# Twelve groups of transposes in an encoder layer, moved from TensorE to DMA

## The chip, the core and the metric

The kernel runs on one core of one Trainium2 chip. The core has a matrix engine (TensorE, PE in the profile), a vector engine (VectorE, DVE), a scalar engine (ScalarE, ACT), a general engine (GpSimd, POOL), a sequencer that mostly issues transfers (SyncE, SP), and 16 DMA engines. Operands lie in SBUF, 128 partitions wide; TensorE writes its results to PSUM, and DMA here moves between HBM and SBUF, or within SBUF. The metric is device time in microseconds of one execution, lower is better.

## What is computed

One layer of a bidirectional encoder on 256 tokens of width 2048, all in float32. Two kinds of attention run side by side on the same projection, and their outputs are gated, merged, projected and followed by an MLP:

```python
h = rms_norm(x, norm_mix_pre[l])
proj = jnp.einsum('bsd,dc->bsc', h, w_in[l])
qa, ka, va, qn, kn, vn, gates = jnp.split(proj, split_at, axis=-1)
...
oa = diff_attention(qa, ka, va, lam)
oa = (rms_norm(oa, subln_w[l]) * (1.0 - lambda_init)).reshape(B, S, DA_WIDTH)
on = neighbourhood_attention(...)
g_a, g_b = jnp.split(jax.nn.sigmoid(gates), N_BRANCHES, axis=-1)
mixed = (g_a * jnp.einsum('bsc,cd->bsd', oa, w_branch_a[l])
         + g_b * jnp.einsum('bsc,cd->bsd', on, w_branch_b[l]))
y = jnp.einsum('bsd,de->bse', mixed, w_out[l])
x = x + rms_norm(y, norm_mix_post[l])
h = rms_norm(x, norm_mlp_pre[l])
u = jnp.square(jax.nn.relu(jnp.einsum('bsd,df->bsf', h, w_up[l])))
x = x + rms_norm(jnp.einsum('bsf,fd->bsd', u, w_down[l]), norm_mlp_post[l])
```

There are four differential heads (called a0 to a3 here), whose weights are `softmax(s1) - lam * softmax(s2)` and whose output is 256 wide, and eight neighbourhood heads (n0 to n7), 128 wide, with a bias and a mask on the scores.

## The kernel before

**Numbers.** Products are made of float32 values split in two parts of a shorter float type, a high and a low one (`hi`, `lo`). ScalarE casts the high part and VectorE subtracts it from the value to get the low one (`parts`, L419; for weights `split`, L138 and L146). A product is then two or three matmuls: for the projections to q and k high times both parts at once (L224, 512 columns) and low times the high part (L226, 256 columns); elsewhere high-high, high-low and low-high (`product3`, L424).

**Projections.** `wgroup` (L215) computes q or k for 512 columns of the weight in four chunks of 4 x 128 rows: 16 pairs of L224 and L226 for one chunk. `agroup` (L258) does v. A chunk's weights are one load of 1 MB on SyncE's queue (L116), then split; raw, high and low parts each have three buffers (pool `wp`, L58). The order is q, k, v for a0 and a1, then for a2 and a3, then for n0 to n3, then for n4 to n7, then the gates, the branch products (`ba`, `bb`), `w_out` and the MLP.

**Heads.** A head is a generator that runs in pieces between the chunks of later projections: `advance` (L204) is called once for a chunk and runs one piece of the head whose turn it is (two from L644 on). A differential head (`diff_head`, L483) has four pieces: the scores and the weights `p`, 2 x 128 x 256, written by L518; `p` transposed (`p_transposed`, L469, called at L522); the product with v (tile `do`), its norm and the scaled output `on` (L544, tile `don` in the profile); and `on` transposed on TensorE (L549, tile `dot`), then scaled and split into `oaT` (L558, L559), which the branch product `ba` reads much later. A neighbourhood head (`na_head`, L564) has three: weights `p` (last written by L597), `p` transposed, and the product with v (tile `no`) with its split into `onT`.

A transposed tile takes four TensorE instructions of 128x128 each, in one PSUM bank, out of which ScalarE and VectorE split it (L421, L422) into `pT`. All these pieces use temporary tiles of 2 KB for a partition (`t2k`, L72), of which there are seven.

**The transposes by DMA that exist.** `sent` (L700) and `joined` (L709) transpose two merged tiles at about 470 us: ScalarE splits float32 into two planes of 16 bits (L704), a DMA on SyncE's queue transposes the planes (L706), and ScalarE joins the two 16-bit halves again (L711). These handle 128 x 2 x 512 values at a time.

**Order.** Nobody writes out the order on each engine. A planner sets it before the run, from the dependences and its own estimate of durations (L36); each engine and each DMA queue then works strictly in that order. Where the program has `issue_after`, an order is forced; the parts touched here have none.

Of the kernel before, what the change touches and what calls it, by code (L numbers as in the profile page):

```python
# [11 lines left out]
F32 = mybir.dt.float32  # L12
F32R = mybir.dt.float32r
U16 = mybir.dt.uint16
AF = mybir.ActivationFunctionType
ALU = mybir.AluOpType
AX = mybir.AxisListType

P = 128
D = 2048  # L20
T = 256
# [30 lines left out]
def encoder_layer(ctx: ExitStack, tc: tile.TileContext, a, out):  # L52
    nc = tc.nc
# [12 lines left out]
    def page(shape, dt, name):  # L66
        return pages.tile(shape, dt, tag="pg", name=name)
# [4 lines left out]
    def t2k(name, dt=F32):  # L72
        return tmp.tile([P, 2, T], dt, tag="t2k", name=name, bufs=7)

    def bank(name, big=False):
        if big:
            return mm.tile([P, 512], F32, tag="mm", name=name)
        return ms.tile([P, 512], F32, tag="ms", name=name)

    def small(w, name):  # L80
        return tiny.tile([P, w], F32, tag=f"s{w}", name=name)
# [13 lines left out]
    def inv_rms(ss, n, name, r=None):  # L95

        w = ss.shape[1]
        ms_ = small(w, f"{name}_m")
        scaled[0] = nc.vector.tensor_scalar(
            ms_, ss, 1.0 / n, EPS, op0=ALU.mult, op1=ALU.add  # L100
        ).ins
        if r is None:
            r = small(w, f"{name}_r")
        nc.gpsimd.tensor_tensor(r, ms_, expo[:, :w], op=ALU.pow)
        return r
# [51 lines left out]
    at = 0  # L157
# [7 lines left out]
    ident = const.tile([P, P], F32, name="ident")  # L165
# [253 lines left out]
    def parts(dst, at, src):  # L419
        hi, lo = dst  # L420
        nc.scalar.copy(hi[at], src)  # L421
        nc.vector.tensor_sub(lo[at], src, hi[at].bitcast(F32))  # L422

    def product3(ps, stat, s_at, mov, m_at, start, stop):  # L424

        for i, (sp, mp) in enumerate(((0, 0), (0, 1), (1, 0))):
            nc.tensor.matmul(
                ps, stat[sp][s_at], mov[mp][m_at], start=start and i == 0, stop=stop and i == 2
            )
# [39 lines left out]
    def p_transposed(p, name):  # L469

        pt = bank(f"{name}_pt")
        for kt in range(2):
            for t in range(2):
                nc.tensor.transpose(
                    pt[:, kt * T + t * P : kt * T + (t + 1) * P],
                    p[:, t, kt * P : (kt + 1) * P],
                    ident,
                )
        r = [t2k(f"{name}_pT{i}", F32R) for i in range(2)]
        parts(r, slice(None), pt.rearrange("p (k q) -> p k q", k=2))  # L480
        return r

    def diff_head(h, qT, kT, v, hl, sc):  # L483
        p = t2k(f"dp{h}")
        for t in range(2):
            s = bank(f"ds{h}{t}")
            for c in range(2):
                product3(
                    s[:, c * T : (c + 1) * T],
                    qT,  # L490
                    (slice(None), hl * 2 + c, slice(t * P, (t + 1) * P)),
                    kT,
                    (slice(None), hl * 2 + c),
                    True,
                    True,
                )
            nb = small(2, f"dnb{h}{t}")
            nc.vector.tensor_reduce(
                nb, s.rearrange("p (c k) -> p c k", c=2), axis=AX.X, op=ALU.max, negate=True
            )  # L500
            nbs = small(2, f"dnbs{h}{t}")
            nc.vector.tensor_scalar_mul(nbs, nb, sc[t])
            e = t2k(f"de{h}{t}")
            z = small(2, f"dz{h}{t}")
            for c in range(2):
                nc.scalar.activation(
                    e[:, c],
                    s[:, c * T : (c + 1) * T],
                    AF.Exp,
                    bias=nbs[:, c : c + 1],  # L510
                    scale=sc[t],
                    accum_out=z[:, c : c + 1],
                )
            rz = small(2, f"drz{h}{t}")
            nc.vector.reciprocal(rz, z)
            nc.vector.tensor_mul(rz[:, 1:2], rz[:, 1:2], lam)
            nc.vector.tensor_scalar_mul(e[:, 1], e[:, 1], rz[:, 1:2])
            nc.vector.scalar_tensor_tensor(  # L518
                p[:, t], e[:, 0], rz[:, 0:1], e[:, 1], op0=ALU.mult, op1=ALU.subtract
            )  # L520
        yield True
        pT = p_transposed(p, f"d{h}")  # L522
        yield True
        o = bank(f"do{h}")
        for t in range(2):
            for kt in range(2):
                product3(
                    o[:, t * T : (t + 1) * T],
                    pT,
                    (slice(None), kt, slice(t * P, (t + 1) * P)),  # L530
                    v,
                    (slice(None), kt, slice(hl * T, (hl + 1) * T)),
                    kt == 0,
                    kt == 1,
                )
        ss = small(2, f"dss{h}")
        on = t2k(f"don{h}")
        for t in range(2):
            nc.scalar.activation(
                on[:, t], o[:, t * T : (t + 1) * T], AF.Square, accum_out=ss[:, t : t + 1]  # L540
            )
        r = inv_rms(ss, 2 * HD, f"dr{h}")
        for t in range(2):
            nc.vector.tensor_scalar_mul(on[:, t], o[:, t * T : (t + 1) * T], r[:, t : t + 1])  # L544
        yield True
        pt = bank(f"dot{h}")
        for eb in range(2):
            for t in range(2):
                nc.tensor.transpose(  # L549
                    pt[:, eb * T + t * P : eb * T + (t + 1) * P],  # L550
                    on[:, t, eb * P : (eb + 1) * P],
                    ident,
                )
        ot = page([P, 2, 512], F32R, f"oaT{h}")
        for eb in range(2):
            src = pt[:, eb * T : (eb + 1) * T]
            g = subs[:, eb : eb + 1]
            nc.scalar.activation(ot[:, eb, :T], src, AF.Copy, scale=g)  # L558
            nc.vector.scalar_tensor_tensor(  # L559
                ot[:, eb, T:], src, g, ot[:, eb, :T].bitcast(F32), op0=ALU.mult, op1=ALU.subtract  # L560
            )
            oT["a", h * 2 + eb] = ot[:, eb]

    def na_head(h, qT, kT, v, hl):  # L564
        p = t2k(f"np{h}")
        s = bank(f"ns{h}")
        for t in range(2):
            product3(
                s[:, t * T : (t + 1) * T],
                qT,  # L570
                (slice(None), hl, slice(t * P, (t + 1) * P)),
                kT,
                (slice(None), hl),
                True,
                True,
            )
        b = bias[h // 2][:, h % 2]
        for t in range(2):
            nc.vector.scalar_tensor_tensor(
                p[:, t],  # L580
                s[:, t * T : (t + 1) * T],
                rxs[:, t : t + 1],
                b[:, 2 - 2 * t : 6 - 2 * t].rearrange("p i c -> p (i c)"),
                op0=ALU.mult,
                op1=ALU.add,
            )
        nb = small(2, f"nnb{h}")
        nc.vector.tensor_reduce(nb, p, axis=AX.X, op=ALU.max, negate=True)
        z = small(2, f"nz{h}")
        for t in range(2):  # L590
            nc.scalar.activation(
                p[:, t], p[:, t], AF.Exp, bias=nb[:, t : t + 1], accum_out=z[:, t : t + 1]
            )
        rz = small(2, f"nrz{h}")
        nc.vector.reciprocal(rz, z)
        for t in range(2):
            nc.vector.tensor_scalar_mul(p[:, t], p[:, t], rz[:, t : t + 1])  # L597
        yield True
        pT = p_transposed(p, f"n{h}")
        yield True  # L600
        o = bank(f"no{h}")
        for kt in range(2):
            product3(
                o[:, :T],
                v,
                (slice(None), kt, slice(hl * P, (hl + 1) * P)),
                pT,
                (slice(None), kt),
                kt == 0,
                kt == 1,  # L610
            )
        if h % 2 == 0:
            oT["nt", h // 2] = page([P, 2, 512], F32R, f"onT{h}")
        ot = oT["nt", h // 2][:, h % 2]
        nc.scalar.copy(ot[:, :T], o[:, :T])
        nc.vector.tensor_sub(ot[:, T:], o[:, :T], ot[:, :T].bitcast(F32))
        oT["n", h] = ot
# [802 lines left out]
    for g in range(2):  # L1420
        pr = Products(f"p{g}", (1, 2, 3, 7))
        pr.in_order = True
        for bi, b in enumerate(blocks[g]):
            end = bi == len(blocks[g]) - 1
            for n, (cg, j, seven) in enumerate(down_steps(g, bi)):
# [42 lines left out]
                for which in range(4):  # L1468
# [4 lines left out]
                    if last:  # L1473
                        bank_, t, half = PLAIN[which]
# [65 lines left out]
```

## Time and profile before

| what | us |
|---|---|
| device time, median of 3 runs | 1337.97 (1337.49 to 1337.99) |
| the profiled execution's own time | 1338.14 |
| its span, first to last instruction | 1336.3 |
| PE busy | 1328.3 |
| DVE busy | 1096.0 |
| ACT busy | 747.7 |

The profile is of one execution. Busy times are sums over an engine's instructions without overlaps; PE's matmuls are pipelined, so a matmul's own duration is longer than the distance to the next one's start. The granted clock of TensorE was 0.998 of full speed. The page names instructions by line of the kernel, engine, operation and tiles, with tile numbers left out: `dp`, `do`, `don`, `dot` belong to the differential heads, `np`, `no` to the neighbourhood heads. In timelines, the first column is the start and the second the length in us, and `[x <-ENGINE tile line]` is the idle time before an instruction and what ended it. SPq and ACTq are the queues' issuing instructions.

### The profile page before, as it was taken

The page shows a single profiled execution, that of the slowest core. Times are in us where ns is not written, and L with a number is a line of the kernel's source. Part 1 is how long each engine was busy: PE and PEld are TensorE (multiplying, and loading weights), DVE is VectorE, ACT ScalarE, POOL GpSimd, SP SyncE. Part 2 cuts the span into 40 slices and gives each one's busy share as a digit, 9 for nine tenths or more (in the row PEclk, how much of TensorE's full clock was granted, in tenths as well). Part 3 has the DMA queues.
Part 4 walks back from the last instruction along what each step waited for, and adds up shares of the span by engine and source line. Part 5 has one row for each costly group of instructions (what it writes and reads, how often), then busy time and mean ns, then how long its engine had stood idle before and what let it go on. Part 6 is the DMA issues. An engine that isn't in the chain of part 4 may idle for free.

```text
span 1336.3 us, 16265 instructions
## 1 busy us (share of the span) xinstructions
PE 1328.3 (99%) x6289; PEld 1112.5 (83%) x6289; DVE 1096.0 (82%) x1275; ACT 747.7 (56%) x873; POOL 39.3 (3%) x73
## 2 busy tenths in 40 slices
PE   9999999999999999999999999999999999999998
PEld 8888888888888888888888888888888888888886
DVE  7978766667787889885688999999978888898886
ACT  6655555545545575555475666666555555555542
POOL 0000000000000000000100000000000000000000
PEclk9999999999999999999999999999999999999999
DMA  9874645564564676567658677877797998698995
GB/s 352 264 228 161 195 165 180 179 192 157 189 217 169 213 220 222 189 220 263 231 182 276 238 250 268 306 238 248 250 361 280 395 385 334 248 371 332 358 351 207
DMA packets 118285, 336.90 MB, mean 252 GB/s; under 512 B 20928, under 2 KB 21440, under 8 KB 118208
## 3 DMA queue, kind: packets, MB, share of 16 engines
q1 hardware_dynamic: 98528, 266.92, 57.9%
q10 hardware_dynamic: 12960, 43.26, 8.4%
q0 software_dynamic: 6720, 25.69, 4.9%
q8 instruction: 49, 0.80, 0.2%
q14 instruction: 28, 0.23, 0.0%
HBM read 307.01 MB, written 29.61 MB: 252 GB/s over the span
## 4 chain that ended last, share of the span: by engine, by line
PE 73%; issue 21%; DMA 3%; DVE 1%; ACT 1%; POOL 0%; POOLq 0%; ACTq 0%
PE u L761 23%; PE ga L761 6%; PE gb L761 6%; PE bb L761 3%; PE ba L761 3%; PE y L761 3%; PE qa_p L224 2%; PE ka_p L224 2%; PE kn_p L224 2%; PE qn_p L224 2%; PE qa_p L226 1%; PE qn_p L226 1%; PE ka_p L226 1%; PE kn_p L226 1%; PE vn_p L267 1%
## 5 line engine op out<-in xcount | busy, mean ns | idle before, releaser
L224 PE MATMUL qn_p<-hT,qn_h 128*128 128x512 f32 x128 | 45.9, 400 | 0.0
L224 PE MATMUL kn_p<-hT,kn_h 128*128 128x512 f32 x128 | 45.6, 400 | 0.0
L224 PE MATMUL ka_p<-hT,ka_h 128*128 128x512 f32 x128 | 45.2, 399 | 0.0
L224 PE MATMUL qa_p<-hT,qa_h 128*128 128x512 f32 x128 | 43.8, 400 | 0.4 <-DVE hT L308 0.4
L761 PE MATMUL u<-u_2h,h2T 128*128 128x512 f32 x128 | 44.0, 396 | 0.0
L761 PE MATMUL u<-u_1h,h2T 128*128 128x512 f32 x128 | 43.4, 389 | 0.0
L761 PE MATMUL u<-u_4h,h2T 128*128 128x512 f32 x128 | 43.3, 391 | 0.0
L761 PE MATMUL u<-u_6h,h2T 128*128 128x512 f32 x128 | 41.0, 389 | 0.0
L761 PE MATMUL u<-u_7h,h2T 128*128 128x512 f32 x128 | 41.0, 389 | 0.0
L226 PE MATMUL qn_p<-hT,qn_l 128*128 128x256 f32 x128 | 35.9, 281 | 0.0
L226 PE MATMUL kn_p<-hT,kn_l 128*128 128x256 f32 x128 | 35.7, 280 | 0.0
L226 PE MATMUL ka_p<-hT,ka_l 128*128 128x256 f32 x128 | 35.2, 282 | 0.0
L226 PE MATMUL qa_p<-hT,qa_l 128*128 128x256 f32 x128 | 32.5, 282 | 0.0
L146 DVE TENSOR_TENSOR y_l<-y_w,y_h 128x1024 fp32r<-128x1024 f32 x16 | 19.0, 1220 | 11.9 <-ACT y_h L138 11.9
L224 PEld LDWEIGHTS kn_p<-hT,kn_h 128*128 128x128 f32 x128 | 24.0, 188 | 5.5
L224 PEld LDWEIGHTS qn_p<-hT,qn_h 128*128 128x128 f32 x128 | 24.1, 188 | 5.3
L146 DVE TENSOR_TENSOR kn_l<-kn_w,kn_h 128x1024 fp32r<-128x1024 f32 x16 | 19.0, 1220 | 11.5 <-ACT kn_h L138 11.5
L224 PEld LDWEIGHTS ka_p<-hT,ka_h 128*128 128x128 f32 x128 | 23.9, 188 | 5.3
L761 PEld LDWEIGHTS u<-u_1h,h2T 128*128 128x128 f32 x128 | 24.0, 188 | 5.0
L146 DVE TENSOR_TENSOR vn_l<-vn_w,vn_h 128x1024 fp32r<-128x1024 f32 x16 | 19.0, 1221 | 11.2 <-ACT vn_h L138 11.2
L761 PEld LDWEIGHTS u<-u_7h,h2T 128*128 128x128 f32 x128 | 24.0, 188 | 5.0
L761 PEld LDWEIGHTS u<-u_6h,h2T 128*128 128x128 f32 x128 | 24.0, 188 | 5.0
(1636 smaller groups left out, 4573.1 us busy)
## 6 DMA issues: line engine op xcount, KB each, us to landing
bh<-keeph ACTq DMA_DIRECT2D x30, 512.0 KB, 9.0
bl<-keepl ACTq DMA_DIRECT2D x30, 512.0 KB, 10.9
keeph<-ah POOLq DMA_DIRECT2D x18, 512.0 KB, 3.8
keepl<-al POOLq DMA_DIRECT2D x18, 512.0 KB, 6.5
va_w<-in_w_in SPq DMA_DIRECT2D x8, 1024.0 KB, 6.4
qn_w<-in_w_in SPq DMA_DIRECT2D x8, 1024.0 KB, 5.1
kn_w<-in_w_in SPq DMA_DIRECT2D x8, 1024.0 KB, 5.0
vn_w<-in_w_in SPq DMA_DIRECT2D x8, 1024.0 KB, 5.0
```

What stands on the lines that cost most here:

```text
L146: sub = nc.vector.tensor_sub(lo[part], src, hi[part].bitcast(F32)).ins
L224: nc.tensor.matmul(ps[b], hi[:, k % 4, cs], mv, start=(k == 0), stop=False)
L226: nc.tensor.matmul(ps[b][:, :T], lo[:, k % 4, cs], mv[:, :T], start=False, stop=(k == nk - 1))
L267: nc.tensor.matmul(ps[t], sh, hi[:, k % 4], start=(k == 0), stop=False)
L761: ins = nc.tensor.matmul(self.ps[i], st, mv[:, blk], start=i not in self.begun, stop=last and n == 2).ins
```

## The change

Heads a0 to a3 and n0 to n3 no longer transpose on TensorE. As soon as a tile (`p`, and for a0 to a3 also `on`) is written, `send` has ScalarE copy it into two planes of 16 bits and a DMA on SyncE's queue transpose them. In the piece where TensorE transposed, `received` has ScalarE join the planes again, and `p_received` then splits the joined tile into `hi` and `lo` from SBUF. That is 12 tiles: 2 for each of four differential heads, 1 for each of four neighbourhood heads, with 4 transposes each, 48 in all. Heads n4 to n7 keep `p_transposed`. The transposed `p` lies as (t, k, q) in place of (k, t, q), for all heads, and the products that read it are written for that. Plane, transfer and join each take a `t2k` tile of the same seven.

```diff
-        r = [t2k(f"{name}_pT{i}", F32R) for i in range(2)]
-        parts(r, slice(None), pt.rearrange("p (k q) -> p k q", k=2))
+        r = [
+            t2k(f"{name}_pT{i}", F32R).rearrange("p t (k q) -> p t k q", k=2) for i in range(2)
+        ]
+        parts(r, slice(None), pt.rearrange("p (k t q) -> p t k q", k=2, t=2))
+        return r
+
+    def send(p, name):
+
+        planes = t2k(f"{name}_s").rearrange("p a b -> p (a b)").bitcast(U16)
+        planes = planes.rearrange("p (t h c) -> p t h c", t=2, h=2)
+        got = t2k(f"{name}_g").rearrange("p a b -> p (a b)").bitcast(U16)
+        nc.scalar.copy(planes, p.bitcast(U16).rearrange("p t (c h) -> p t h c", h=2))
+        nc.sync.dma_start(
+            got.rearrange("p (b q) -> p b q", q=P),
+            planes.rearrange("p t h c -> p (t h c)"),
+            transpose=True,
+        )
+        return got
+
+    def received(got, name):
+
+        r = t2k(name)
+        nc.scalar.copy(
+            r.bitcast(U16).rearrange("p t (c h) -> p t h c", h=2),
+            got.rearrange("p (t h c) -> p t h c", t=2, h=2),
+        )
+        return r.rearrange("p t (k q) -> p t k q", k=2)
+
+    def p_received(got, name):
+
+        pT = received(got, f"{name}_pT")
+        r = [
+            t2k(f"{name}_pT{i}", F32R).rearrange("p t (k q) -> p t k q", k=2) for i in range(2)
+        ]
+        parts(r, slice(None), pT)
         return r
...
@@ diff_head
+        got = send(p, f"dp{h}")
         yield True
-        pT = p_transposed(p, f"d{h}")
+        pT = p_received(got, f"d{h}")
         yield True
...
-                    (slice(None), kt, slice(t * P, (t + 1) * P)),
+                    (slice(None), t, kt),
...
+        got = send(on, f"do{h}")
         yield True
-        pt = bank(f"dot{h}")
-        for eb in range(2):
-            for t in range(2):
-                nc.tensor.transpose(
-                    pt[:, eb * T + t * P : eb * T + (t + 1) * P],
-                    on[:, t, eb * P : (eb + 1) * P],
-                    ident,
-                )
+        oT_ = received(got, f"dot{h}")
         ot = page([P, 2, 512], F32R, f"oaT{h}")
         for eb in range(2):
-            src = pt[:, eb * T : (eb + 1) * T]
+            src = oT_[:, :, eb]
...
@@ na_head
+        got = send(p, f"np{h}") if h < 4 else None
         yield True
-        pT = p_transposed(p, f"n{h}")
+        pT = p_received(got, f"n{h}") if got is not None else p_transposed(p, f"n{h}")
         yield True
         o = bank(f"no{h}")
         for kt in range(2):
             product3(
-                o[:, :T],
+                o[:, :T].rearrange("p (t q) -> p t q", t=2),
                 v,
                 (slice(None), kt, slice(hl * P, (hl + 1) * P)),
                 pT,
-                (slice(None), kt),
+                (slice(None), slice(None), kt),
```

More of the change, by code (lines that the diff above doesn't have):

```diff
@@ L544, in diff_head @@
             nc.vector.tensor_scalar_mul(on[:, t], o[:, t * T : (t + 1) * T], r[:, t : t + 1])
+        got = send(on, f"do{h}")
         yield True
-        pt = bank(f"dot{h}")
-        for eb in range(2):
-            for t in range(2):
-                nc.tensor.transpose(
-                    pt[:, eb * T + t * P : eb * T + (t + 1) * P],
-                    on[:, t, eb * P : (eb + 1) * P],
-                    ident,
-                )
+        oT_ = received(got, f"dot{h}")
         ot = page([P, 2, 512], F32R, f"oaT{h}")
         for eb in range(2):
-            src = pt[:, eb * T : (eb + 1) * T]
+            src = oT_[:, :, eb]
             g = subs[:, eb : eb + 1]
-            nc.scalar.activation(ot[:, eb, :T], src, AF.Copy, scale=g)
+            hi, lo = (
+                ot[:, eb, at * T : (at + 1) * T].rearrange("p (t q) -> p t q", t=2) for at in range(2)
+            )
+            nc.scalar.activation(hi, src, AF.Copy, scale=g)
             nc.vector.scalar_tensor_tensor(
-                ot[:, eb, T:], src, g, ot[:, eb, :T].bitcast(F32), op0=ALU.mult, op1=ALU.subtract
+                lo, src, g, hi.bitcast(F32), op0=ALU.mult, op1=ALU.subtract
             )
```

## Prediction

> **What bounds the kernel now.** I read the page's busy rows first, then the view of who waits for whom, for PE alone.
>
> ```profile
> span 1336.3 us, 16265 instructions
> PE 1328.3 (99%) x6289; PEld 1112.5 (83%) x6289; DVE 1096.0 (82%) x1275; ACT 747.7 (56%) x873; POOL 39.3 (3%) x73
> ```
>
> ```profile
> PE x_last L1373 <- ACT by_rows L1370: 2.2, 1, 2.2
> ```
>
> TensorE is busy for 1328.3 of 1336.3 us, so 8.0 us of the whole execution are left in which it stands. Its longest wait on anybody, 2.2 us, lies in the last microseconds of the kernel. A busy PE need not be a full one, so I looked at the three stretches that the change touches, in the view by stage. After the first column the columns are length, busy time and instruction count of PE, PEld, DVE, ACT and POOL, granted clock, DMA share, GB/s.
>
> ```profile
> 74.00:126.00 52.00, 52.00 (x316) 46.02 (x315) 41.75 (x82) 28.13 (x57) 1.43 (x2) 1.00 0.58 180
> 147.00:200.00 53.00, 53.00 (x323) 47.01 (x322) 36.61 (x70) 28.56 (x59) 1.65 (x2) 1.00 0.52 167
> 222.00:292.00 70.00, 70.00 (x398) 61.09 (x397) 47.26 (x77) 36.23 (x62) 0.00 (x0) 1.00 0.58 185
> ```
>
> Heads a0 and a1 run in the first stretch, a2 and a3 in the second, n0 to n3 in the third. PE has no gap in any of them; VectorE is busy 80%, 69% and 68% of the time, ScalarE 54%, 54% and 52%, the DMA engines 52 to 58%. The bound is the PE's own instruction stream. Whatever leaves it is worth its place in the stream, so long as nothing put in its stead makes PE wait.
>
> **What is removed.** Heads a0 to a3 lose two groups of four transposes each, n0 to n3 one: 12 groups, 48 transposes.
>
> ```profile
> L474 PE MATMUL d_pt<-ident,dp x16: 270/272/273, 87.5 to 171.2; 128*128 128x128 f32 x16
> ```
>
> ```profile
> 113.37 0.28 PE L226 MATMUL ka_p<-hT,ka_l 128*128 128x256 f32 x1
> 113.48 0.40 PE L224 MATMUL ka_p<-hT,ka_h 128*128 128x512 f32 x1
> 113.72 0.28 PE L226 MATMUL ka_p<-hT,ka_l 128*128 128x256 f32 x1
> 113.85 0.60 PE L549 MATMUL dot<-ident,don 128*128 128x128 f32 x4
> 114.20 0.48 PE L224 MATMUL ka_p<-hT,ka_h 128*128 128x512 f32 x1
> 114.52 0.28 PE L226 MATMUL ka_p<-hT,ka_l 128*128 128x256 f32 x1
> ```
>
> The 272 ns of the first row is how long one transpose is in the pipeline, not what it keeps from others. For that I read starts: from L226 to the next L226, with one L224 between, takes 113.72 - 113.37 = 0.35 us without transposes and 114.52 - 113.72 = 0.80 us with four. A group costs 0.45 us in the stream, 0.11 each; the merged row agrees, four in 0.60 us of which the last 0.27 is drain. Reading starts to a hundredth leaves 0.43 to 0.45. I take 0.44: 12 x 0.44 = **5.3 us** off PE.
>
> The Trainium skill speaks against the change here. The page "VectorE: DVE Perf Modes", section "Rules for kernel authors", says to transpose 128x128 on TensorE if the result may lie in PSUM, and by DMA otherwise; its section "The three transpose paths" gives 390 ns against 1309 ns. The trace differs on the first figure, 0.11 us in a full stream; by 390 ns the estimate of the gain would be 48 x 0.39 = 18.7 us. A single block by DMA no row here shows.
>
> **What is added on ScalarE.** The kernel makes two transposes of this sort already, for the merge, on twice the size:
>
> ```profile
> L704 ACT COPY m_s<-ga x4: 1037/1042/1042, 467.2 to 470.0; 128x1024 uint16<-128x1024 uint16 x4
> L706 SPq DMA_TRANSPOSE m_g<-m_s x2: 1692/2418/3145, 469.2 to 472.4; - x2
> ```
>
> ```profile
> L711 ACT COPY m<-m_g x2: 2514/2524/2533, 481.9 to 489.4; 128x2048 uint16<-128x2048 uint16 x2
> ...
> DMA to landing us min/median/max: 3.9/4.6/5.3
> ```
>
> A split here is 128x1024 uint16, 1.04 us as in L704; a join is half of L711, 1.26 us. Twelve of each are 12 x 2.30 = 27.6 us, 9.2 us in each stretch. ScalarE rises from 28.1 to 37.3 of 52 us, from 28.6 to 37.8 of 53, and from 36.2 to 45.4 of 70. It stays below three quarters, with idle time to hold them, so on the path I put nothing. Without that cover it would be all 27.6.
>
> The evacuations keep their count; they read SBUF in place of PSUM. For L421 and L422 at 128x512:
>
> ```profile
> L421 ACT CAST d_pT<-d_pt x4: 570/576/587, 89.5 to 171.5; 128x512 fp32r<-128x512 f32 x4
> L422 DVE TENSOR_TENSOR d_pT<-d_pt,d_pT x4: 680/682/684, 90.9 to 172.2; 128x512 fp32r<-128x512 f32 x4
> ```
>
> No row shows these shapes from SBUF. Were each half as long or half as long again, that would be 12 x 0.3 us on either engine, inside the idle time above. I count zero.
>
> **What is added on SyncE and DMA.** Twelve transposes of 256 KB. The nearest row issues in 1.7 to 3.1 us and lands in 3.9 to 5.3 us at 512 KB; I take the whole 5.3 for half the size, with half as the lower bound. Weight loads behind one on the queue are delayed by some 2 us, and have room for it:
>
> ```profile
> 71.57 0.37 SPq L116 DMA_DIRECT2D ka_w<-in_w_in  x1
> ...
> 85.08 0.37 SPq L116 DMA_DIRECT2D ka_w<-in_w_in  x1
> 85.49 0.56 SPq L371 DMA_DIRECT2D skew<-in_rpbp  x1
> 91.03 0.37 SPq L116 DMA_DIRECT2D ka_w<-in_w_in  x1
> ```
>
> ```profile
> ka_w<-in_w_in SPq DMA_DIRECT2D x7, 1024.0 KB, 6.6
> ```
>
> ```profile
> 87.56 2.00 ACT L138 CAST ka_h<-ka_w 128x1024 fp32r<-128x1024 f32 x2 [0.27 <-PE qa_p L224]
> ...
> 93.65 2.00 ACT L138 CAST ka_h<-ka_w 128x1024 fp32r<-128x1024 f32 x2 [3.62 <-PE qa_p L224]
> ```
>
> The load of 71.57 is there at about 78.2 and is cast at 87.56: 9.4 us of room. The casts themselves wait for PE to leave a buffer; with three buffers a chunk so cast is due two chunks later, 2 x 16 x 0.35 = 11 us, of which cast and subtraction take 4.5. So a stall of up to about 6 us of ScalarE costs PE nothing there.
>
> **The wait that takes the place of the transposes.** A join stands on ScalarE until its transfer has landed, and PE's product with p (L427, tile do) waits for join, cast and subtraction. When p is ready, and when PE uses it:
>
> ```profile
> 83.43 0.48 DVE L518 SCALAR_TENSOR_TENSOR dp<-de,drz 128x256 f32<-128x256 f32 x1
> ...
> 88.11 0.49 DVE L518 SCALAR_TENSOR_TENSOR dp<-de,drz 128x256 f32<-128x256 f32 x1
> ```
>
> ```profile
> 99.66 1.60 PE L427 MATMUL do<-va,d_pT 128*128 128x256 f32 x12
> ...
> 103.93 1.60 PE L427 MATMUL do<-va,d_pT 128*128 128x256 f32 x12
> ...
> 159.97 0.48 DVE L518 SCALAR_TENSOR_TENSOR dp<-de,drz 128x256 f32<-128x256 f32 x1
> ...
> 166.67 0.48 DVE L518 SCALAR_TENSOR_TENSOR dp<-de,drz 128x256 f32<-128x256 f32 x1
> ...
> 174.10 1.60 PE L427 MATMUL do<-va,d_pT 128*128 128x256 f32 x12
> ```
>
> ```profile
> 179.78 1.49 PE L427 MATMUL do<-va,d_pT 128*128 128x256 f32 x11
> ...
> 247.18 0.60 DVE L597 TENSOR_SCALAR np<-np,nrz 128x256 f32<-128x256 f32 x2
> ...
> 290.37 0.88 PE L427 MATMUL no<-n_pT,vn 128*128 128x256 f32 x6
> ```
>
> The room for a0, a1, a2, a3 is 99.66 - 83.91 = 15.7, 103.93 - 88.60 = 15.3, 174.10 - 160.45 = 13.6 and 179.78 - 167.15 = 12.6 us; for n3, the last of its four, 42.6 us. The second product of a0 to a3, with `oaT`, comes only in stage ba, over 100 us later. The new path is 1.04 (split) + 5.3 (transfer) + 1.26 (join) + 0.58 (cast) + 0.68 (subtraction) = 8.9 us. So 3.7 to 6.8 us are left for queueing, and I take no wait.
>
> The diff also makes `pT` lie as (t, k, q), so the 24 products of n0 to n3 read their moving operand in two runs of 128, and so do the 24 of n4 to n7. No row shows that. Bounds: nothing, or as if each were two instructions of 128 at the transposes' 0.11 each in place of one L226 at 0.11 to 0.12, 48 x 0.10 = 4.8 us. I take nothing, as the number of columns is the same. A gain is excluded for that reason.
>
> **Sum.** 1336.3 - 5.3 = 1331.0 us of span. The profiled execution took 1338.14 us, 1.8 more than its span and 0.2 above the median of 1337.97; against the median I predict 1337.97 - 5.3 = **1332.7 us**. About 0.2%, 2.7 us, is what a measurement of this kernel can tell from no change.
>
> **The rivals.**
> - *The path to p is longer than it looks (slower).* SyncE works in order. If a transpose is put behind a weight load that waits for its buffer, it waits up to one spacing, 85.08 to 91.03 or about 6 us. The path is then 14.9 us and the heads are late by 0, 0, 1.3 and 2.3. If split and join each also stand behind one double cast (2.00 us) on ScalarE, it is 18.9, and they are late by 3.2, 3.6, 5.3 and 6.3: 18.4 us, which gives 1332.7 + 18.4 = 1351. It decides from the point where the lateness sums to 5.3, a path of about 15.6 us. For it: both queues are in order and planned beforehand. Against: ScalarE's idle half, and a transfer half as large as the one I price it by.
> - *The gain is mostly eaten (no change).* Either the first half of that, lateness of 3 to 5 us, or the two-run operand at its upper bound of 4.8 us: 1336 to 1337.5. Or PE is only seemingly the bound in stretch one, where VectorE works 80% of the time and the change relieves it of next to nothing; then the removal does not do what it says, and the time stays at 1338. Against this last: PE's starts stand 0.35 apart without gaps.
> - *A transpose is worth its whole duration.* 48 x 0.272 = 13.1 us, 1324.9. The starts 0.11 apart speak against it. The page "TensorE: Matmul & The Clock Gate" of the Trainium skill, section "PE-mode transpose", gives about 275 ns in one kernel's context, which agrees with the 272 as a duration; by it as a price the estimate is 13.2 us.
>
> **How the numbers follow.** Forecast 0.70, with its own range 1331.5 to 1335: the gain between 3 and 6.5 us. Eaten 0.14. Slower 0.12. Whole duration 0.04. Faster is 0.70 + 0.04 = 0.74, same 0.14, slower 0.12. The range takes in the forecast and the eaten case, 0.84 together: 1331.5 to 1338.
>
> **What would show it.** Right: 48 fewer PE transposes, 16 left on L474 and none on L549's old place; twelve DMA transposes more; PE still full in all three stretches, no wait of `do` or `no` for `d_pT` or `n_pT`, and every later stage starting 5 us earlier. Splits of 1.04 and joins of 1.26 us on ScalarE, and `no` starts still 0.11 to 0.12 apart. Wrong: gaps on PE ahead of `do` in stretch one or two, ScalarE idle before a join with a DMA as its releaser while casts stand behind it, or landings of much more than 5.3 us.

## Result and profile after

The changed kernel takes 1333.94 us (median of 7 runs, 1332.97 to 1335.31), the kernel before 1337.82 beside it (7 runs, 1337.49 to 1337.99). The ratio is 0.9973, 95% interval 0.9963 to 0.9982: 3.9 us faster, where 5.3 were forecast. The runs also spread more, over 2.3 us in place of 0.5.

The profiled execution of after is the slowest of its seven, 1335.31 us. Its page, busy rows:

```profile
span 1333.5 us, 16224 instructions
PE 1322.1 (99%) x6241; PEld 1106.0 (83%) x6241; DVE 1097.0 (82%) x1275; ACT 773.2 (58%) x897; POOL 39.2 (3%) x73
```

PE has 48 instructions fewer and is busy 6.2 us less, but its span is only 2.8 us shorter: it stands for 11.4 us in place of 8.0. ScalarE has 24 instructions more, 25.5 us. The six longest waits in the view of waits, PE alone, of after:

```profile
PE x_last L1405 <- ACT by_rows L1402: 2.2, 1, 2.2
PE uT L1233 <- ACT u L1251: 1.0, 1, 1.0
PE idle L174 <- POOL ones L164: 1.0, 1, 1.0
PE qa_p L224 <- DVE hT L308: 0.9, 1, 0.9
PE p L793 <- DMA bl<-keepl: 0.8, 1, 0.8
PE vn_p L267 <- DVE sc_s L294: 0.4, 1, 0.4
```

None of these is a wait of `do` or `no` for the transposed p. Four are new or longer than before, where `uT` and `qa_p` have 0.4 each. Of these, `qa_p` lies ahead of the change, `vn_p` lies in the heads, and `uT` and `p` lie in the MLP, hundreds of us behind the change. To see where time came and went I use the **lead**: how much earlier a matmul starts than the same one in the profile of before. The view by tile of before (lengths in ns, then first and last start), and below it PE's timeline of before:

```profile
L761 PE MATMUL u<-u_1h,h2T x128: 387/389/397, 648.3 to 960.2; 128*128 128x512 f32 x128
```

```profile
1066.08 0.39 PE L761 MATMUL p<-d050h,bl 128*128 128x512 f32 x1
...
1330.65 2.08 PE L1373 MATMUL x_last<-zg,by_rows 128*128 128x256 f32 x4 [2.19 <-ACT by_rows L1370]
```

The same two views of after:

```profile
L793 PE MATMUL u<-u_1h,h2T x128: 387/389/397, 643.6 to 955.5; 128*128 128x512 f32 x128
```

```profile
1062.90 0.50 PE L793 MATMUL p<-d050h,bl 128*128 128x512 f32 x1 [0.79 <-DMA bl<-keepl]
...
1327.61 1.37 PE L1405 MATMUL x_last<-zg,by_rows 128*128 128x256 f32 x4 [2.19 <-ACT by_rows L1402]
```

The lead is 4.7 us at the first product of w_up and still 4.7 at 960, then 3.2 at 1066 and 3.0 at the end. So the heads brought 4.7 to 4.8, and 1.7 were given back between 995 and 1067 us. Followed through the heads in the same way, matmul by matmul, the lead of after is -0.1 at 60 us, 1.9 at 126, 2.9 at 198 and 4.8 at 300. Four groups were removed in each stretch; the middle one brought only 1.0. There the timeline of after shows a gap at the step from k to v, before which the last k banks are emptied:

```profile
196.50 0.40 PE L224 MATMUL kn_p<-hT,kn_h 128*128 128x512 f32 x1
196.74 0.28 PE L226 MATMUL kn_p<-hT,kn_l 128*128 128x256 f32 x1
197.42 0.50 PE L267 MATMUL vn_p<-vn_h,hT 128*128 128x512 f32 x1 [0.39 <-DVE sc_s L294]
197.75 0.40 PE L268 MATMUL vn_p<-vn_l,hT 128*128 128x512 f32 x1
```

Next starts should be 0.12 after 196.74 and 0.23 after 197.42, and are 0.68 and 0.33 after: 0.66 us lost. ScalarE in the same microseconds:

```profile
191.58 1.36 ACT L501 COPY dot<-do_g 128x1024 uint16<-128x1024 uint16 x1 [0.79 <-DMA do_g<-do_s]
192.81 1.99 ACT L138 CAST vn_h<-vn_w 128x1024 fp32r<-128x1024 f32 x2
194.71 0.90 ACT L589 ACTIVATE oaT<-dot,subs 128x256 fp32r<-128x256 f32 x2
195.51 0.88 ACT L292 COPY sc_r<-kn_p 128x256 f32<-128x256 f32 x3
```

A join waits 0.79 us for its transfer, and behind it stand a weight cast, the scaling of the joined tile (`oaT`) and only then the copies of the k banks. These copies end at 196.39. What PE waits for, by its own row, is the addition L294 on VectorE that empties the banks, and there the joined tile stands ahead as well:

```profile
193.88 2.36 DVE L146 TENSOR_TENSOR vn_l<-vn_w,vn_h 128x1024 fp32r<-128x1024 f32 x2 [2.57 <-ACT vn_h L138]
196.15 0.88 DVE L590 SCALAR_TENSOR_TENSOR oaT<-dot,subs,oaT 128x256 fp32r<-128x256 f32 x2
196.95 1.08 DVE L294 TENSOR_TENSOR sc_s<-kn_p,sc_r 128x256 f32<-128x256 f32 x3
```

The new instructions themselves, from the views by tile of after:

```profile
L490 ACT COPY dp_s<-dp x4: 1041/1046/1047, 84.0 to 168.0; 128x1024 uint16<-128x1024 uint16 x4
L491 SPq DMA_TRANSPOSE dp_g<-dp_s x4: 1232/1277/1354, 85.1 to 169.1; - x4
...
DMA to landing us min/median/max: 2.7/4.2/5.5
```

```profile
L427 PE MATMUL do<-va,d_pT x48: 273/283/288, 98.9 to 182.1; 128*128 128x256 f32 x48
L501 ACT COPY d_pT<-dp_g x4: 1357/1364/1379, 95.2 to 174.3; 128x1024 uint16<-128x1024 uint16 x4
L421 ACT CAST d_pT<-d_pT x4: 620/625/647, 96.7 to 175.7; 128x512 fp32r<-128x512 f32 x4
L422 DVE TENSOR_TENSOR d_pT<-d_pT,d_pT x4: 685/692/693, 97.3 to 176.3; 128x512 fp32r<-128x512 f32 x4
```

For a0 the subtraction ends at 98.0 and PE's product starts at 98.9. The path fits, with 0.9 us to spare, since the planner put the join late (95.2, where the transfer issued at 85.1 had landed by 90.6 at the latest).

**Theory A**: a group is worth some 0.47 us of PE's stream and comes through in full; 0.7 are lost in the heads to evacuations held up behind a join, and what reaches the MLP is partly lost where the DMA engines are full. **Rival B**: a group is worth only 3.9 / 12 = 0.32 us. **Rival C**: the late loss comes from something fixed, such as the order planned there.

### The profile page after: what moved, and what is told of

It is laid out like the page before. It is cut to its first block, busy times and chain, and to the rows that moved or that the text cites. A ratio compares the mean times of both kernels' runs of the same rounds, so it can differ in the third digit from the quotient of the medians.

```text
span 1333.5 us, 16224 instructions
## 1 busy us (share of the span) xinstructions
PE 1322.1 (99%) x6241; PEld 1106.0 (83%) x6241; DVE 1097.0 (82%) x1275; ACT 773.2 (58%) x897; POOL 39.2 (3%) x73
## 4 chain that ended last, share of the span: by engine, by line
PE 72%; issue 21%; DMA 3%; DVE 2%; ACT 1%; POOL 0%; SPq 0%; POOLq 0%; ACTq 0%
PE u L793 23%; PE ga L793 6%; PE gb L793 6%; PE ba L793 3%; PE bb L793 3%; PE y L793 3%; PE qn_p L224 2%; PE ka_p L224 2%; PE kn_p L224 2%; PE qa_p L224 2%; PE qn_p L226 1%; PE ka_p L226 1%; PE vn_p L267 1%; PE vn_p L268 1%; PE y_p L269 1%
## 5 line engine op out<-in xcount | busy, mean ns | idle before, releaser
L224 PEld LDWEIGHTS qa_p<-hT,qa_h 128*128 128x128 f32 x128 | 23.5, 188 | 5.7 <-ACT qa_h L144 1.1
L793 PEld LDWEIGHTS u<-u_4h,h2T 128*128 128x128 f32 x128 | 24.0, 188 | 4.9
```

Of the source, the lines that this page charges most:

```text
L224: nc.tensor.matmul(ps[b], hi[:, k % 4, cs], mv, start=(k == 0), stop=False)
L793: ins = nc.tensor.matmul(self.ps[i], st, mv[:, blk], start=i not in self.begun, stop=last and n == 2).ins
```

## The experiments

Each kernel was timed beside the kernel before, whose median was 1337.57, 1337.74 and 1337.75 us in the three comparisons (e1 to e4, e5 to e8, e9 to e12). Leads are those of each run's profiled execution against the profile of before, worked out from PE's timelines, at the first gate product (300 us), at 990 and at the end; it varies by some tenths already at 60 us, ahead of every edit (0.2 to -0.3, and -0.6 in e12).

| run | median us | range | difference to before | lead 300 / 990 / end |
|---|---|---|---|---|
| changed kernel | 1333.94 | 1332.97 to 1335.31 | -3.9 | 4.8 / 4.7 / 3.0 |
| e1 again | 1333.71 | 1332.84 to 1336.60 | -3.9 | 4.7 / 4.6 / 3.3 |
| e2 p alone | 1335.46 | 1334.33 to 1336.89 | -2.1 | 3.7 / 3.8 / 4.0 |
| e3 output tile alone | 1336.28 | 1336.07 to 1336.98 | -1.3 | 1.7 / 1.7 / 1.7 |
| e4 late join | 1333.51 | 1332.72 to 1335.16 | -4.1 | 5.6 / 5.3 / 3.2 |
| e5 before, fewer reloads | 1337.60 | 1337.32 to 1337.96 | -0.1 | 0.2 / 0.2 / 0.6 |
| e6 changed, fewer reloads | 1333.57 | 1332.91 to 1333.66 | -4.2 | 5.0 / 5.0 / 5.5 |
| e7 both paths | 1338.22 | 1337.88 to 1338.47 | +0.5 | -0.2 / -0.2 / 0.3 |
| e8 all heads, late join | 1345.81 | 1345.27 to 1346.43 | +8.1 | 5.4 / -8.4 / -7.9 |
| e9 late join, fewer reloads | 1332.62 | 1332.23 to 1333.20 | -5.1 | 5.5 / 5.4 / 5.9 |
| e10 p alone, fewer reloads | 1334.03 | 1333.61 to 1334.64 | -3.7 | 3.7 / 3.7 / 4.2 |
| e11 transposes twice | 1345.57 | 1344.91 to 1346.09 | +7.8 | -5.5 / -8.3 / -7.9 |
| e12 layout alone | 1337.69 | 1337.51 to 1338.31 | -0.1 | -0.6 / -0.6 / -0.1 |

**e1, the changed kernel again.** No edit.

> The changed kernel once more, for its spread and a second profile. Lead means how much earlier a stage's first matmul starts than in the profile of before. Theory A: each removed group of four is worth 0.47 us on TensorE; 0.6 to 0.7 us are lost at one place, the step from k to v of the third projection (about 197 us), and up to 1.7 us in the stretch from 995 to 1066 us where the DMA engines are full, more in some executions than in others. Then the lead is again 4.7 to 4.8 at the first gate product, and whatever is lost between 995 and 1070 us varies from execution to execution; median 1333.4 to 1334.4. Rival B: a group is worth only 3.9 / 12 = 0.32 us; then the lead at the first gate product is 3.9. Rival C: the late loss is fixed by the planned order; then the same 0.6 and 1.1 us are lost at the same two matmuls.

The lead is 4.65 at the gates, so B falls. The late loss is not at the same places: at 999 us this execution lost nothing, and gained 0.5 on the profile of before, which had waited there itself; at the matmul with `bl` it lost 1.8. C as "the same two losses" falls too.

**e2, p alone.** The output tile goes back to TensorE:

```diff
-        got = send(on, f"do{h}")
         yield True
-        oT_ = received(got, f"dot{h}")
+        pt = bank(f"dot{h}")
+        for eb in range(2):
+            for t in range(2):
+                nc.tensor.transpose(...)
```

> Only p goes by DMA, 8 groups; the output tile of the differential heads is transposed on TensorE as before. Theory A: no loss at 197 us, so the lead at the first gate product is 8 x 0.47 = 3.8 less 0.1 or 0.2, and the time 1334.1 to 1335.2, almost that of the whole change. Rival B, 0.32 us for each group: lead 2.6, time 1335.3.

The lead of 3.7 fits A (8 groups, 0.45 each from the 0.1 at 60 us), the time does not: 1335.46, where 3.7 us would be 1333.9; by the time alone, B's 1335.3 would be nearer. The profiled execution, 1334.33, was the fastest of the eleven and shows no late loss; the median run must have lost some 1.1 us more that no profile shows.

**e3, the output tile alone.** `send` and `p_received` for p are taken back in both kinds of heads.

> Only the output tile goes by DMA, 4 groups; all p stay on TensorE. Theory A: 4 x 0.47 = 1.9 less the loss of 0.66 at 197 us, lead 1.2 at the first gate product, time 1336.6 or a little above. If the loss at 197 us does not come from these joins: lead 1.9, time 1336.0. Rival B: lead 1.3, with no gap on TensorE at 197 us.

Lead 1.65 and no gap at 197 us, so a join of this tile is not enough for the gap. The order fits that: here the evacuations of the joined tile were planned ahead of the weight cast (192.79 and 194.40 on ScalarE), and those of the k banks directly behind the weight's split, on ScalarE and on VectorE.

**e4, late join.** A second `yield True` between `send(on, ...)` and `received`.

> The whole change, with the join of the output tile put one piece (two chunks of the projection) later. If the join of the fourth differential head holds up ScalarE's evacuation of the k banks at 197 us, the gap of 0.66 there goes and the lead at the first gate product is 5.4, time 0.6 below the changed kernel's. If the gap has another cause, the lead stays 4.8 and the time the same.

The gap is gone and the lead at the gates is 5.6. Timelines of e4, PE, then ScalarE, then VectorE:

```profile
196.57 0.28 PE L226 MATMUL kn_p<-hT,kn_l 128*128 128x256 f32 x1
196.69 0.40 PE L267 MATMUL vn_p<-vn_h,hT 128*128 128x512 f32 x1
```

```profile
192.77 1.99 ACT L138 CAST vn_h<-vn_w 128x1024 fp32r<-128x1024 f32 x2
194.66 0.63 ACT L292 COPY sc_r<-kn_p 128x256 f32<-128x256 f32 x2
```

```profile
196.11 1.08 DVE L294 TENSOR_TENSOR sc_s<-kn_p,sc_r 128x256 f32<-128x256 f32 x3
```

The join itself did not move: the planner put it at 191.54, against 191.58 in the changed kernel, with the weight cast behind it at 192.77 against 192.81. What the second `yield` moved is the evacuation of the joined tile, which now starts at 199.87. So the copies of the k banks follow the cast at 194.66 in place of 195.51, and VectorE's addition follows the weight's subtraction at 196.11 in place of 196.95. The cause of the gap is thus the joined tile's evacuation ahead of that of the k banks, on VectorE above all, and not the join alone. How much the join adds by making the weight's split late was not tried. The time hardly moved: 1333.51 against 1333.71 in the same comparison, with ranges that overlap. The profile lost 2.4 us of lead on the way, most of it behind 990.

**e5 and e6, fewer reloads.** The down projection reloads activations that were kept in HBM (`bh`, `bl`). Where four of these reloads are left out, the DMA engines have room:

```diff
-                        if not end:
+                        if g == 0 and bi in (0, 1, 2, 3):
+                            sets[g, blocks[g][bi + 1] + c] = sets[g, blocks[g][bi] + c]
+                        elif not end:
                             sets[g, blocks[g][bi + 1] + c] = act_again(blocks[g][bi + 1] + c, g)
```

> The kernel before with less traffic in the down projection: for the first half of the columns, the second to fifth blocks reuse the activations of the block before them in place of reloading (four reloads of two sets fewer, between about 980 and 1160 us; these blocks' products are of other activations than the reference's). Reference for the next run. Theory A: TensorE hardly waits there in the kernel before (0.4 us at 999), so 1337.0 to 1337.6. If the full DMA engines held back the kernel before as well, it is faster by 1 us or more.

> The changed kernel with the same reloads left out. Theory A: what is lost behind 995 us is lost to the full DMA engines, so the lead of 4.7 us at the first gate product is still there at the last product, the time is 1332.4 to 1332.9 and its spread under 1 us. Rival C (the planned order, or anything else that does not depend on this traffic): 0.6 to 1.7 us are lost as before, time 1333.5 to 1334 with a spread of 2 us or more.

The kernel before hardly gains (0.1 us). The changed kernel keeps its whole lead of 5.0 behind 990 us, gains the 0.5 that before had lost, and its spread shrinks to 0.75 us. The views by stage of before, of after and of e6 (columns as in the prediction), for the same stretches:

```profile
980.00:1000.00 20.00, 19.57 (x89) 15.99 (x88) 14.88 (x14) 12.13 (x13) 1.06 (x2) 1.00 1.01 383
1040.00:1060.00 20.00, 20.00 (x90) 16.56 (x89) 17.47 (x15) 10.69 (x8) 0.53 (x1) 1.00 1.03 415
```

```profile
980.00:1000.00 20.00, 18.96 (x86) 15.45 (x85) 12.53 (x12) 9.29 (x8) 0.55 (x2) 1.00 1.01 378
1020.00:1040.00 20.00, 20.00 (x90) 16.55 (x89) 17.07 (x19) 11.11 (x12) 3.19 (x6) 1.00 1.02 403
1040.00:1060.00 20.00, 20.00 (x90) 16.58 (x89) 19.17 (x16) 11.54 (x9) 0.00 (x0) 1.00 1.00 394
```

```profile
980.00:1000.00 20.00, 20.00 (x93) 16.37 (x92) 14.14 (x14) 10.47 (x9) 1.06 (x2) 1.00 0.70 248
1020.00:1040.00 20.00, 20.00 (x89) 16.54 (x89) 17.70 (x15) 11.55 (x9) 2.12 (x4) 1.00 0.93 315
1040.00:1060.00 20.00, 20.00 (x90) 16.57 (x89) 19.44 (x18) 11.55 (x9) 0.00 (x0) 1.00 0.68 234
```

In before and in after the DMA engines are busy all the time, at up to 415 and 403 GB/s; in e6 they are not, and PE has no gap.

The wait at `uT` can be followed to a load that e6 does not touch. ScalarE, of after:

```profile
992.37 1.91 ACT L710 CAST d0120h<-d0120r 128x2048 fp32r<-128x2048 f32 x1 [2.46 <-DMA d0120r<-in_w_down]
994.19 1.94 ACT L1251 ACTIVATE u<-u,r 128x512 f32<-128x512 f32 x3
```

The cast waits for a weight load of 1 MB, and behind it stands the `u` for which PE waits. This load took 13.8 us to land in after and 13.3 in before, and 6.2 in e6, though it was issued no sooner in e6 (979.2) than in after (978.5). In e1 it landed at 991.2, 1.1 us sooner than in after, and PE did not wait. The wait at `bl` is another matter, as e6 leaves out that very reload, so that there is nothing left to wait for. What the traces show of it is that after issued it 4.1 us earlier than before (1046.7 against 1050.8) and that it landed only 2.3 us earlier (1062.9 against 1065.2).

The median, 1333.57, missed A's 1332.4 to 1332.9 and lies in C's 1333.5 to 1334; lead and spread are as A said. Only the profiled execution, 1332.91, comes near in time. Some 0.7 us of this kernel's ordinary runs are not explained.

**e7, both paths.** The kernel before with its transposes, and `send` and `received` beside them.

> The kernel before with all its TensorE transposes, and in addition every split, DMA transpose and join of the change, whose joined tiles nobody reads. Theory A: the additions cost nothing but the evacuation held up at 197 us and perhaps a like place, 0.5 to 1.5 us: 1338.1 to 1339.1. Rival: the additions cost more than that in many small waits, then 1340 or more; or nothing at all, then 1337.6.

The additions cost 0.5 us in the median and 0.4 to 0.5 of lead in the heads (0.2 at 60 us, -0.2 at 300). The gap at the step from k to v, which A expected here too, is not there: PE goes on from 200.38 to 200.49. Neither B's missing 1.8 us nor more is in them. The interval of the ratio, 0.9994 to 1.0012, includes no cost at all.

**e8, all heads and the late join.** `if h < 4 else None` is dropped from e4.

> The changed kernel with the late join of the output tile, and the last four neighbourhood heads by DMA as well: 16 groups. Theory A: lead at the first branch product 5.6 + 4 x 0.47 = 7.5 us, of which 1 to 2 are lost behind 995 us: 1331.0 to 1332.0. Rival: with two pieces for each chunk the joins of the last four heads come too soon after their transfers, TensorE waits ahead of their products with v, and the lead at the first branch product is 6 or less.

Slower by 8 us, by another wait than the rival named. PE, view of waits and timeline of e8:

```profile
PE ba L794 <- ACT ga L970: 12.7, 1, 12.7
```

```profile
339.13 1.59 PE L427 MATMUL no<-n_pT,vn 128*128 128x256 f32 x12
353.42 0.79 PE L794 MATMUL ba<-ba_0h,oaT 128*128 128x512 f32 x1 [12.71 <-ACT ga L970]
```

```profile
350.75 0.62 ACT L869 CAST hs<-hs6s 128x512 fp32r<-128x512 f32 x1 [0.96 <-DVE hs6s L867]
351.39 1.28 ACT L970 ACT_TABLE_LOAD   x1
352.68 2.42 ACT L970 ACTIVATE ga<-ga,rx 128x512 f32<-128x512 f32 x4
```

PE has finished the gate and waits for its four banks, which only the sigmoid on ScalarE frees. In the order planned here the sigmoids stand behind the joins of the last heads and behind casts of `hs`. VectorE writes the sources of those between 339 and 350 us, after the last subtractions of transposed p. `hf` and the heads' planes, transfers and joins share the seven `t2k` buffers; that this is why `hs` came so late was not tried by itself. Of the two edits, only the four heads touch this stretch.

The wait is not the whole loss. The view by stage of e8:

```profile
340.00:354.00 14.00, 1.29 (x8) 1.02 (x7) 13.52 (x33) 6.85 (x11) 0.00 (x0) 0.69 0.39 139
354.00:364.00 10.00, 10.00 (x35) 8.04 (x34) 2.36 (x2) 2.98 (x4) 0.00 (x0) 0.75 0.00 0
```

The granted clock is 0.75 in the 10 us after the wait and 1.00 again from 364. The products of `ba` start 0.43 us apart from 354.0 to 358.7, and 0.23 apart behind that, as in before. For the 12 products up to 358.7 that is some 2.6 us more.

**e9 and e10, late join and p alone with fewer reloads.** The edit of e6 on e4 and on e2.

> The late join of e4 with the reloads left out as in e6 (again products of other activations there). The late join gained 0.8 us of lead at the gates and nothing in the time. If the full DMA engines behind 995 us take what it gains: the lead of 5.6 stays to the end, and the time is 0.6 to 0.8 below e6, 1332.8 to 1333.0. If the 0.8 is lost to something else: same as e4, 1333.4 or more.

> The eight groups of p alone (e2), with the reloads left out. E2 had a lead of 3.7 at the gates but a median only 2.1 below before. If the full DMA engines take the difference: 1337.6 - 3.7 = 1333.9, at most 1334.2. If not: 1335.2 to 1335.5 as in e2.

Both did what theory A expects of the full DMA engines. With room on them the late join is worth 1333.57 - 1332.62 = 0.95 us in the medians, more than the 0.6 to 0.8 expected and more than the 0.5 between the leads; without room it was worth 0.2. P alone is 1334.03 in place of 1335.46, and keeps its 3.7.

**e11, transposes twice.** `for kt in (0, 1, 0, 1)` and `for eb in (0, 1, 0, 1)` in the kernel before.

> The kernel before with every transpose of the heads made twice into the same place: 16 groups of four more on TensorE, nothing else added. If a group costs its place in the stream, 0.44 to 0.47 us: 7.0 to 7.5 more, 1344.7 to 1345.3. If a transpose costs its duration of 0.272: 17.4 more, 1355.

+7.8 us, 0.49 for each of 16 groups and 0.3 above the expected range; the lead falls from -0.28 at 60 us to -7.26 at 345, which is 0.44 each, and another 1.1 go later, 0.7 of it in a wait of PE at `ba`. A transpose is worth its place in the stream, 0.11 us, not its 0.27.

**e12, layout alone.** (t, k, q) with all transposes on TensorE.

> The kernel before with the transposed p laid as (t, k, q) and the products written for it, all transposes on TensorE. Nothing: 1337.5 to 1337.9. If an operand in two runs of 128 cost like two instructions: 4.8 more, 1342.5.

Nothing, 1337.69 against 1337.75. An operand in two runs of 128 costs no more than one of 256.

## Why the prediction was right, and where its size was off

- *The bound and the price.* Right. PE's stream was the bound, and 0.44 us for a group was near: 0.44 in e11, 0.42 to 0.46 by the leads of e2, e3 and e9. In the changed kernel it is 0.46: its lead from 60 to 300 us grew by 4.9, and 0.7 were lost in between, 5.5 us for 12 groups where the sum has 5.3. The rival by the whole duration falls with e11. So do, as prices in a full stream, the 390 ns (of bf16) of the Trainium skill's page "VectorE: DVE Perf Modes" (section "The three transpose paths") and the 275 ns of its page "TensorE: Matmul & The Clock Gate" (section "PE-mode transpose"): the measured 0.11 us decides.
- *ScalarE.* Splits took 1.05 us as forecast, joins 1.36 in place of 1.26, casts from SBUF 0.62 in place of 0.58. The busy time rose by 25.5 us in place of 27.6. "On the path I put nothing" failed by 0.7 us, the 0.66 at 197 us. I had weighed ScalarE's idle time and the depth of the weight buffers, but not the order: the joined tile's evacuation, on ScalarE and on VectorE, came ahead of that of the PSUM banks at the step from one projection to the next, which has no such depth. E4, which moved that evacuation and left the join, had no gap. So PE was not full in all three stretches (52.61 of 53.00 us in the second), and a sign that I had named as wrong was there: ScalarE idle before a join, with a DMA as its releaser and a cast behind it. By itself that sign meant little, since ScalarE also stood for 1.32 us before a join at 252 us, with a cast behind it, and PE has no gap there.
- *The path to p.* Right that it fits: PE never waited for it. Landings were 2.7 to 5.7 us, at most 0.4 above my price for half the size. The slower rival did not happen: on SyncE's queue the transpose stood ahead of the weight load (issued at 85.1, the load behind it).
- *The two runs of 128.* Nothing, as taken (e12).
- *"Every later stage starting 5 us earlier."* This is the step that failed most. It was 4.7 up to 990 us and then less, because there the DMA engines are full and PE's earlier start meets transfers that do not all come as much earlier. I read the DMA share only in the three stretches of the heads, where it was 52 to 58%; the profile of before shows 1.01 and 1.03 in the stretches above. E6, e9 and e10 show it: without part of that traffic, the profiles keep their whole lead, and the weight load behind the wait at `uT` lands in 6.2 us in place of 13.8. In medians, each against the kernel before and less the 0.1 us that the edit gives to that kernel, leaving out this traffic brought 1.5 us for p alone, 0.9 for the late join and only 0.2 for the changed kernel itself. It also took away most of the added spread.

In sum: 5.5 removed, 0.7 lost in the heads, about 0.9 lost later, 3.9 left. Of the 0.9, 0.2 is put down to the DMA engines by the medians of e5, e6 and e1; the two profiled executions of the changed kernel lost 1.7 and 1.3 there. The remaining 0.7 stays open: ordinary runs of e6 are that much above what its profile would give, and no profile shows where.

## What to carry to other kernels

On a full engine, price an instruction by the distance it puts between its neighbours' starts, not by its duration. When work leaves the bound, look at every later stage for one that has no slack to follow: a stretch of full DMA engines can give back hundreds of us later part of what was gained, and here it also showed as a wider spread. The DMA share over the whole span, read before the change, would have pointed to it. Work put on an in-order engine that is idle on average can still cost the bound: what counts is which short-lived buffer, here a PSUM bank, is emptied behind it.

## What the runs showed of the hardware that was not expected

The subtraction of L422 took 0.69 us from SBUF and 0.68 from PSUM, and the cast of L421 0.62 against 0.58: moving the source out of PSUM gained nothing. Issuing a transpose by DMA held SyncE's queue for 1.23 to 1.35 us at 256 KB, once for 2.20, where a 1 MB load between them took 0.37 to 0.54. In e8, PE stood for 12.7 us and its granted clock was 0.75 in the next 10; it was 1.00 there in before. In the stretch of full DMA engines a 1 MB load took 13.8 us to land, against 6.2 with part of the traffic left out.
